# FFN's side 12 in two pieces: one k tile at the weights' place modulo 256 bytes, three 192 bytes beyond

## The chip, the core and the metric

The kernel runs on one core of a Trainium2 chip. The core has TensorE (PE, the matrix engine; its loads of the stationary operand are listed apart as PEld), VectorE (DVE), ScalarE (ACT), GpSimd (POOL) and SyncE (SP, which only issues transfers). Data lie in SBUF, 128 partitions wide, and matmul results in PSUM banks. The metric is the device time of one execution in microseconds; a time before the change is the median of three runs.

## The reference

A trunk of four layers over 512 positions and 1024 channels, in float32. Each layer adds a mixer and then a gated feed-forward network (FFN) to `x`:

```python
for layer in range(DEPTH):                      # DEPTH = 4
    h = rmsnorm(x, norm_mix[layer])
    # layers 0 and 3: s5_mixer; 1: gla_mixer; 2: diff_attn_mixer
    x = x + mix
    h = rmsnorm(x, norm_ffn[layer])
    x = x + swiglu_ffn(h, ffn_w_gate_up[layer], ffn_w_down[layer])
return rmsnorm(x, norm_final)

def swiglu_ffn(h, w_gate_up, w_down):
    g, u = jnp.split(h @ w_gate_up, 2, axis=-1)  # 1024 x (2 x 2816)
    return (jax.nn.silu(g) * u) @ w_down         # 2816 x 1024
```

The change is in `h @ w_gate_up` of all four layers.

## The kernel before

**Numbers in two parts.** A float32 product is made of three matmuls in the format `float32r`: each operand is split into a high part (a cast on ACT) and a low part (a subtraction on DVE), and high x high, high x low and low x high are summed in PSUM. For weights this is `high` (line 405) and `low` (line 413), which fill one of five buffers `whl`. One matmul takes a stationary operand of 128 x 128, loaded just before it, and a moving operand of 256 or 512 columns.

**The FFN's first product with seven multiplications.** `h` transposed and the weights are each taken as 2 x 2 blocks, and the product is made by a scheme with seven block products in place of eight (Strassen's kind). The 2816 hidden columns go in 11 blocks of 256 (`seven_block`). A block takes seven products with the names `one` to `seven`. Each product has 24 matmuls (line 576): two column halves `j`, four k tiles of 128, and the three part products, with the weights stationary and a *side* moving, 256 columns wide. Sides are sums of quarters of `h`: "11" and "12" are quarters themselves, "1", "2", "3", "4" and "22" are others or sums. Products `one`, `six`, `seven` and `four` write the PSUM bank `a`, `five` and `three` bank `c`, and `two`, the only one that reads side "12", writes `d`, a bank of another group (`sbank`, tag "s"). From block 2 on the order in a block is `one`, `five`, `six`, `two`, `seven`, `three`, `four`.

**Where sides lie.** Sides "11" and "12" lie in one tile `sides` of 4160 float32 columns. It is a slot of the pool `hp`, of 16,640 bytes a partition, which is 65 x 256, so that both slots of that pool start at the same place modulo 256. In the tile, side "11" starts at column 48 (192 bytes) and side "12" at column 2112 (8448 bytes, 33 x 256). Each holds high and low part (`z`), four k tiles and 256 columns; the steps between these are multiples of 256 bytes. The other five sides have tiles of their own, in the FFN's pool. The pieces of `whl` that are loaded as weights all start at multiples of 256 bytes from its start.

**How sides 11 and 12 are made.** While the mixer before the FFN ends, `Sides.take` scales each half tile of `x` with the gains, PE transposes it, and `keep` copies it (line 196) into the tile `halves`. When the second of the four position tiles is in, `parts` splits the quarter: a cast on ACT (line 192) and a subtraction on DVE (line 193), each of 128 x 1024. This happens twice per layer, for "11" and for "12".

**The order of work.** The first two blocks of an FFN follow a plan that is written out (the string `plan` in `ffn`: products of block `a` and `b`, splits of weights, sums of sides); there, and in the last steps of the mixer that lead to it, every engine's order is by hand (`hand_all`). From there on (`hand()`) a planner orders the instructions by their place in the program and the costs it assumes. After three or four blocks a group ends, and `gemm_b` (lines 433 to 435) multiplies the activations of the group with the down projection, 512 columns wide, into the banks `acc`. In layer 0 groups have 3, 3, 3 and 2 blocks, in the others 4, 4 and 3. The attention's own value projection has a 256-column form of its own (`values_of`, line 2378), in which `hT` is stationary and `whl` moves, into banks `acc`.

Weights come by DMA, 512 KB at a time, issued on SP, and where a sum of two quarters is wanted, a second one is added by a DMA of POOL (line 612).

Of the kernel before, what the change touches and what calls it, by code (L numbers as in the profile page):

```python
# [12 lines left out]
F32 = mybir.dt.float32  # L13
# [4 lines left out]
ALU = mybir.AluOpType  # L18
# [50 lines left out]
class Left:  # L69
# [15 lines left out]
    def room(self):  # L85
        self.hT = [self.tr.hp.tile([P, KT, SEQ], F32R, tag="hT", name=f"hT{z}") for z in range(2)]
# [67 lines left out]
class Sides(Left):  # L154
# [6 lines left out]
    def room(self):  # L161
        F = self.tr.hp.tile([P, 4, 4, 256], F32, tag="hT", name="halves")
        self.whole = F
        self.F = {(0, 0): F[:, 0], (1, 0): F[:, 1], (0, 1): F[:, 2], (1, 1): F[:, 3]}

        two = self.tr.hp.tile([P, 4096 + 64], F32R, tag="hT", name="sides")
        at = lambda n: two[:, n : n + 2048].rearrange("p (z k n) -> p z k n", z=2, k=4)
        self.place = {"11": at(48), "12": at(2112)}
        self.heads = []

    def quarter(self, q, half, b):
# [15 lines left out]

        return [self.F[k] for k in ((0, 0), (0, 1), (1, 0), (1, 1))]

    def parts(self, name, src, ks=slice(0, 4)):  # L190
        o = self.place[name][:, :, ks]
        self.tr.nc.scalar.copy(o[:, 0], src)
        self.tr.nc.vector.tensor_tensor(o[:, 1], src, o[:, 0].bitcast(F32), op=ALU.subtract)

    def keep(self, t, d, p):
        self.tr.nc.scalar.copy(self.F[t // 2, d][:, :, (t % 2) * P : (t % 2 + 1) * P], p[:])
# [129 lines left out]
class Trunk:  # L326
# [236 lines left out]
        return evac  # L563


    def seven_product(self, side, w, bank, first, hl=None):

        if hl is None:
            hl = self.halves(w, 4, 256)
        mm = self.nc.tensor.matmul  # L570
        for j in range(2):
            c = slice(j * P, (j + 1) * P)
            o = bank[:, j * 256 : (j + 1) * 256]
            for k in range(4):
                for n, (x, y) in enumerate(((0, 0), (0, 1), (1, 0))):
                    mm(  # L576
                        o, hl[:, x, k, c], side[:, y, k], start=first and not (j or k or n),
                        stop=k == 3 and n == 2, skip_group_check=True,
                    )

    def seven_block(self, fp, slots, left, wgu, b, turn, na):
# [1 line left out]

        nc = self.nc
        v = nc.vector
        A = left.place
        T = lambda name: fp.tile([P, 512], F32, tag="r1" if name == "r1" else "glu", name=name, bufs=2 if name == "r1" else 3)
        W, H, bank, keep, lent = {}, {}, {}, {}, set()
        if b < 2:
# [40 lines left out]
        def room1(room=None):  # L630
            load("1", 0, 1, (0, 0), room)

        def room22(room=None):
            load("22", 1, 1, None, room)
# [2 lines left out]
            load("3", 0, 1, (1, 1))  # L637

        def product(side, name, bank, first):
            self.seven_product(A[side], W.get(name), bank, first, H.pop(name, None))  # L640

        def one():
            bank["a"] = self.acc("a")
            product("11", "11", bank["a"], True)
# [5 lines left out]
        def two():  # L650
            bank["d"] = self.sbank("d")
            product("12", "21", bank["d"], True)
# [7 lines left out]
        def five():  # L660
            bank["c"] = self.acc("c")
            product("1", "1", bank["c"], True)
# [59 lines left out]
    def ffn(self, l, left, after=None, turn=False, aside=None, small=None):  # L722
# [7 lines left out]
        with self.tc.tile_pool(name=f"ffn{l}", bufs=1, reuse_waits="tile") as fp:  # L730
# [6 lines left out]
            if glued:  # L737
                lent = room()
# [1801 lines left out]
```

## Time and profile before

| | |
|---|---|
| median of 3 runs | 2264.95 us (2261.33 to 2266.5) |
| the profiled execution | 2264.01 us |
| its span, first to last instruction | 2262.1 us |
| mean granted TensorE clock | 0.996 |
| busy: PE, DVE, ACT, POOL | 97%, 70%, 49%, 14% |
| matmuls of line 576 in all four layers | 7392, of which 1056 read side 12 |

One execution was recorded with the profiler. A row of a group of instructions gives its line, engine and operation, the tiles written and read (`d<-sides,whl`), the shape, the count, then busy time in us, mean duration in ns, and the idle time of the engine ahead of it with what ended most of it. A row of the timeline gives start, us from start to last end, engine, line, tiles and count. A row of the chain gives the start, the length and the work that the end of the kernel is followed back to. Times are from the span's start. Ends of matmuls are modelled, and matmuls overlap.

### The profile page before, as it was taken

Reading aid. Unit: us, or ns where it says so; the run is one execution under the profiler, and the core shown is the slowest. Engines: PE = TensorE matmul, PEld = TensorE weight load, DVE = VectorE, ACT = ScalarE, POOL = GpSimd, SP = SyncE. Lnnn points to the kernel's source line nnn. Section 1 sums busy time; section 2 is a strip of 40 time slices with the busy share of each in tenths; the row PEclk is TensorE's granted clock in tenths of the full one; section 3 lists DMA queues with packets and bytes.
Section 4 is the critical chain, followed back from the end, with each engine's and each line's share of the span. In section 5 each row is a group of like instructions: output and inputs, shape, how many; then the busy total and the mean of one; then the engine's idle time right before and its main releaser. Section 6 shows DMA issues by size and latency. Waiting matters only on the chain.

```text
span 2262.1 us, 37360 instructions
## 1 busy us (share of the span) xinstructions
PE 2191.7 (97%) x14967; PEld 1963.9 (87%) x14967; DVE 1580.2 (70%) x2411; ACT 1111.5 (49%) x1773; POOL 317.9 (14%) x432
## 2 busy tenths in 40 slices
PE   6999999999999999999999999999999899999998
PEld 5888889989777799998988888989998788989997
DVE  9955878776535488776745676967766965957675
ACT  8534535444443365564435676644544234635443
POOL 4301141431000010100002231101000000101000
PEclk9999999999999999999999999999999999999999
DMA  4356666763322566765237465985641546766632
GB/s 89 65 170 167 172 159 176 173 172 100 106 76 74 149 158 178 180 172 154 94 137 149 100 152 138 237 212 134 174 99 50 153 146 155 198 160 161 165 75 75
DMA packets 295527, 319.92 MB, mean 141 GB/s; under 512 B 70141, under 2 KB 235289, under 8 KB 295226
## 3 DMA queue, kind: packets, MB, share of 16 engines
q1 hardware_dynamic: 232730, 235.79, 34.5%
q0 software_dynamic: 62624, 81.75, 19.5%
q8 instruction: 118, 1.93, 0.4%
q14 instruction: 55, 0.45, 0.1%
HBM read 285.62 MB, written 16.65 MB: 134 GB/s over the span
## 4 chain that ended last, share of the span: by engine, by line
PE 48%; DVE 3%; ACT 2%; issue 1%; DMA 1%; POOL 0%; DVEq 0%; POOLq 0%; ACTq 0%; SPq 0%
PE a L576 10%; PE acc L433 8%; PE acc L435 8%; PE acc L434 8%; PE c L576 5%; PE d L576 3%; PE y L1481 1%; PE op L2323 1%; PE s L2290 1%; DVE whl L413 1%; PE acc L2378 1%; ACT whl L405 1%; PE V L1445 1%; PE tp L116 0%; DMA wst<-in_ffn_w_gate_up_dram 0%
## 5 line engine op out<-in xcount | busy, mean ns | idle before, releaser
L413 DVE TENSOR_TENSOR whl<-wst,whl 128x1024 fp32r<-128x1024 f32 x272 | 331.6, 1223 | 276.9 <-ACT whl L405 276.2
L405 ACT CAST whl<-wst 128x1024 fp32r<-128x1024 f32 x272 | 284.6, 1051 | 339.7 <-PE acc L435 250.3
L576 PE MATMUL a<-side,whl 128*128 128x256 f32 x3168 | 383.9, 277 | 6.9 <-DVE whl L413 6.0
L576 PEld LDWEIGHTS a<-side,whl 128*128 128x128 f32 x3168 | 371.0, 188 | 9.2 <-DVE whl L413 6.7
L433 PE MATMUL acc<-whl,act 128*128 128x512 f32 x704 | 276.4, 393 | 1.7 <-DVE g L621 1.2
L434 PE MATMUL acc<-whl,act 128*128 128x512 f32 x704 | 275.0, 391 | 0.0
L435 PE MATMUL acc<-whl,act 128*128 128x512 f32 x704 | 274.9, 390 | 0.0
L576 PE MATMUL c<-side,whl 128*128 128x256 f32 x2112 | 255.2, 277 | 3.3 <-DVE whl L413 3.3
L576 PEld LDWEIGHTS c<-side,whl 128*128 128x128 f32 x2112 | 247.0, 188 | 4.2 <-DVE whl L413 4.1
L413 DVE TENSOR_TENSOR whl<-slot,whl 128x1024 fp32r<-128x1024 f32 x105 | 127.7, 1221 | 67.3 <-ACT whl L405 66.9
L433 PEld LDWEIGHTS acc<-whl,act 128*128 128x128 f32 x704 | 132.5, 188 | 30.8 <-DVE g L621 1.7
L435 PEld LDWEIGHTS acc<-whl,act 128*128 128x128 f32 x704 | 132.4, 188 | 27.6
L405 ACT CAST whl<-slot 128x1024 fp32r<-128x1024 f32 x105 | 110.0, 1052 | 92.5 <-PE acc L435 41.2
L434 PEld LDWEIGHTS acc<-whl,act 128*128 128x128 f32 x704 | 132.4, 188 | 26.4 <-issue 0.2
L576 PE MATMUL d<-sides,whl 128*128 128x256 f32 x1056 | 133.7, 283 | 2.5 <-ACT whl L405 2.5
L576 PEld LDWEIGHTS d<-sides,whl 128*128 128x128 f32 x1056 | 128.9, 191 | 3.3 <-ACT whl L405 3.3
L576 PE MATMUL a<-sides,whl 128*128 128x256 f32 x1056 | 129.3, 278 | 1.2 <-DVE whl L413 1.2
L433 PE MATMUL acc<-whl,hT 128*128 128x512 f32 x320 | 128.6, 402 | 0.0
L576 PEld LDWEIGHTS a<-sides,whl 128*128 128x128 f32 x1056 | 125.2, 188 | 2.4 <-DVE whl L413 1.4
L435 PE MATMUL acc<-whl,hT 128*128 128x512 f32 x320 | 125.3, 392 | 0.0
L434 PE MATMUL acc<-whl,hT 128*128 128x512 f32 x320 | 125.3, 391 | 0.0
L612 POOL DMA_DIRECT2D wst<-in_ffn_w_gate_up_dram x44 | 57.0, 1295 | 443.9 <-DMA wst<-in_ffn_w_gate_up_dram 222.7
(456 smaller groups left out, 3935.1 us busy)
## 6 DMA issues: line engine op xcount, KB each, us to landing
wst<-in_ffn_w_gate_up_dram SPq DMA_DIRECT2D x88, 512.0 KB, 4.6
wst<-in_ffn_w_down_dram SPq DMA_DIRECT2D x88, 512.0 KB, 4.4
slot<-in_ffn_w_gate_up_dram SPq DMA_DIRECT2D x69, 512.0 KB, 5.7
wst<-in_ffn_w_gate_up_dram POOLq DMA_DIRECT2D x44, 512.0 KB, 6.2
halves<-in_ffn_w_gate_up_dram SPq DMA_DIRECT2D x42, 512.0 KB, 5.0
wst<-in_s_w_glu_dram SPq DMA_DIRECT2D x32, 512.0 KB, 4.9
wst<-in_gla_w_in_dram SPq DMA_DIRECT2D x24, 512.0 KB, 3.7
wst<-in_diff_w_qkv_dram SPq DMA_DIRECT2D x24, 512.0 KB, 4.6
```

The source lines that it names most:

```text
L405: self.last["high"] = self.nc.scalar.copy(hl[:, 0], w[:])
L413: self.last["low"] = self.nc.vector.tensor_tensor(hl[:, 1], w[:], hl[:, 0].bitcast(F32), op=ALU.subtract)
L433: mm(out, lh, rh, start=first, stop=False)
L434: mm(out, lh, rl, start=False, stop=False)
L435: self.last["mm"] = mm(out, ll, rh, start=False, stop=last)
L576: mm(o, hl[:, x, k, c], side[:, y, k], start=first and not (j or k or n), stop=k == 3 and n == 2, skip_group_check=True,)
L612: nc.gpsimd.dma_start(w[:], left.quarter(*plus, b), accum_op=ALU.add)
L1445: mm(V[kk][z][:, bs(b)], inm[:, z, bs(b)], U[:, bs(b)], start=True, stop=True)
L1481: mm(yb[:, b], q[:, j, b], om[:, j // 2, bs(b)], start=False, stop=j == 3)
L2290: nc.tensor.matmul(ss[m][:], qs[:, m, ts], ks[:, m, z], start=z == 0, stop=z == 1)
L2323: nc.tensor.matmul(op[:, 0], aT[:, kt], vall[0][:, kt, j * P : (j + 1) * P], start=kt == 0, stop=kt == 3)
L2378: nc.tensor.matmul(o, stat(k, x, t), hl[:, y, a], start=not (k or t % 2 or n), stop=k == KT - 1 and n == 2, skip_group_check=True,)
```

## The change

Side 11 moves to column 560 of its tile (2240 bytes, 8 x 256 + 192). Side 12 is stored in two pieces: k tile 0 at column 0 (512 columns: high and low part), and k tiles 1 to 3 at column 2608 (10,432 bytes, 40 x 256 + 192; 1536 columns). `parts` makes it with one cast and one subtraction for each piece, both casts ahead of both subtractions. The products fetch a moving slice through a new function `row`, which picks the piece by k tile. Nothing is changed in the attention: its order of before, which the change's title calls mended, is in both kernels.

```diff
         two = self.tr.hp.tile([P, 4096 + 64], F32R, tag="hT", name="sides")
-        at = lambda n: two[:, n : n + 2048].rearrange("p (z k n) -> p z k n", z=2, k=4)
-        self.place = {"11": at(48), "12": at(2112)}
+        at = lambda n, k=4: two[:, n : n + 512 * k].rearrange("p (z k n) -> p z k n", z=2, k=k)
+        self.place = {"11": at(560)}
+        self.split12 = [(slice(0, 1), at(0, 1)), (slice(1, 4), at(2608, 3))]
...
-    def parts(self, name, src, ks=slice(0, 4)):
-        o = self.place[name][:, :, ks]
-        self.tr.nc.scalar.copy(o[:, 0], src)
-        self.tr.nc.vector.tensor_tensor(o[:, 1], src, o[:, 0].bitcast(F32), op=ALU.subtract)
+    def parts(self, name, src):
+        pieces = self.split12 if name == "12" else [(slice(0, 4), self.place[name])]
+        for ks, o in pieces:
+            self.tr.nc.scalar.copy(o[:, 0], src[:, ks])
+        for ks, o in pieces:
+            self.tr.nc.vector.tensor_tensor(o[:, 1], src[:, ks], o[:, 0].bitcast(F32), op=ALU.subtract)
+
+    def row(self, name, z, k):
+
+        if name != "12":
+            return self.place[name][:, z, k]
+        return self.split12[0][1][:, z, 0] if k == 0 else self.split12[1][1][:, z, k - 1]
...
-    def seven_product(self, side, w, bank, first, hl=None):
+    def seven_product(self, row, w, bank, first, hl=None):
...
-                        o, hl[:, x, k, c], side[:, y, k], start=first and not (j or k or n),
+                        o, hl[:, x, k, c], row(y, k), start=first and not (j or k or n),
...
-        A = left.place
...
         def product(side, name, bank, first):
-            self.seven_product(A[side], W.get(name), bank, first, H.pop(name, None))
+            row = lambda y, k: left.row(side, y, k)
+            self.seven_product(row, W.get(name), bank, first, H.pop(name, None))
```

## Prediction

> **What bounds the kernel now.** I read the page first: the span, the busy shares, the chain that ended last and the costliest groups. The columns of a group are its instructions, then busy us and mean ns of one, then the idle time before them.
>
> ```profile
> span 2262.1 us, 37360 instructions
> PE 2191.7 (97%) x14967; PEld 1963.9 (87%) x14967; DVE 1580.2 (70%) x2411; ACT 1111.5 (49%) x1773; POOL 317.9 (14%) x432
> PE 48%; DVE 3%; ACT 2%; issue 1%; DMA 1%; POOL 0%; DVEq 0%; POOLq 0%; ACTq 0%; SPq 0%
> L576 PE MATMUL d<-sides,whl 128*128 128x256 f32 x1056 | 133.7, 283 | 2.5 <-ACT whl L405 2.5
> ```
>
> TensorE (PE) is busy 97% of the span, and nearly all of the chain that the profile could follow is PE. `d` is the bank of product `two`, the only product that reads side 12; there are 44 of them (1056 / 24). Where they stand I read from stretches that hold whole FFN blocks from the third on; of nine such stretches (29 of the 44 `d` lie in them) here are the first and the sum:
>
> ```profile
> core 0: us, PE busy (x) PEld busy (x) DVE busy (x) ACT busy (x) POOL busy (x), PEclk, DMA share, GB/s
> 323.85:381.80 57.95, 57.95 (x506) 57.95 (x505) 44.66 (x50) 32.30 (x40) 6.42 (x7) 1.00 0.72 188
> ...
> sum 560.49, PE 560.49 PEld 560.44 DVE 428.31 ACT 300.63 POOL 45.14; mean PE 62.28 PEld 62.27 DVE 47.59 ACT 33.40 POOL 5.02
> ```
>
> PE is busy in all of the 560.49 us, at clock 1.00, and VectorE (DVE) in 76%. So a nanosecond saved per matmul here is a nanosecond of the kernel until DVE is late, which has a quarter of the time to spare. The timeline of PE shows what a matmul costs. The start of one product minus the start of the next is the figure to trust, since durations overlap (2.88 us of records in 2.72 us):
>
> ```profile
> 323.62 0.39 PE L435 MATMUL acc<-whl,act 128*128 128x512 f32 x1
> 323.85 2.99 PE L576 MATMUL a<-sides,whl 128*128 128x256 f32 x24
> 326.68 2.99 PE L576 MATMUL c<-side,whl 128*128 128x256 f32 x24
> 329.50 2.99 PE L576 MATMUL a<-side,whl 128*128 128x256 f32 x24
> 332.33 3.04 PE L576 MATMUL d<-sides,whl 128*128 128x256 f32 x24
> 335.20 2.90 PE L576 MATMUL a<-side,whl 128*128 128x256 f32 x24
> 337.94 2.88 PE L576 MATMUL c<-side,whl 128*128 128x256 f32 x24
> ...
> 348.82 2.88 PE L576 MATMUL a<-side,whl 128*128 128x256 f32 x24
> 351.54 3.02 PE L576 MATMUL d<-sides,whl 128*128 128x256 f32 x24
> 354.40 2.90 PE L576 MATMUL a<-side,whl 128*128 128x256 f32 x24
> 357.14 1.07 PE L576 MATMUL c<-side,whl 128*128 128x256 f32 x8
> ```
>
> Three paces are in it. A product takes 2.72 us (348.82 to 351.54; 113.3 ns a matmul): **fast**. After the wide `acc` matmuls the same products take 2.83 us (323.85 to 326.68; 117.8 ns): **slow**, and they stay so, product after product, until a `d` comes. `d` takes 2.86 us (351.54 to 354.40; near 120 ns), and the product behind it 2.74. After every whole `d` the pace is fast, also where it was slow before. So `d` does two things: it costs 2.86 + 2.74 - 2 x 2.72 = 0.16 us more than two fast products, and it ends the slow pace.
>
> By the code, side 12 begins 2112 x 4 = 8448 = 33 x 256 bytes into its tile, the place of the weights modulo 256 by the change's own words; side 11 begins 192 bytes beyond, and runs at the fast or the slow pace. That the place is what costs has a second witness. In the attention, line 2378 multiplies `hT` and `whl` slices that both start at their tiles' place (all steps are multiples of 256 bytes), and it writes `acc` banks. Its median is that of `d`, where the fast products have 276 (second row):
>
> ```profile
> L2378 PE MATMUL acc<-whl,hT x192: 274/283/365, 1281.6 to 1337.6; 128*128 128x256 f32 x192
> L576 PE MATMUL a<-sides,whl x1056: 276/276/384, 214.2 to 2205.3; 128*128 128x256 f32 x176
> ```
>
> **The change part by part.**
>
> *Product `two`.* Of 24 matmuls, the 6 of k tile 0 (three in each column half) stay at the weights' place; 18 go 192 bytes beyond. 24 matmuls at the place cost 0.16 us, 6.7 ns each; so 6 cost 0.04 us if the cost goes with their number. Saved per `d`: 0.12 us. The ends: 0.16 if three in a row are too few to build the delay up, 0.08 if each first half leaves the nine matmuls behind it slow (9 x 4.5 ns).
>
> *Which of the 44 count.* The 29 in the nine stretches do. Of the 7 `d` of the blocks just ahead of these, I count the 5 of layers 0, 1 and 3. Two come early in each layer, under the written plan. There the chain of layer 3 reads:
>
> ```profile
> 1923.11 5.74 PE d L576 x48
> ...
> 1937.03 0.91 PE rows L147 x8
> ...
> 1939.09 0.96 ACT whl L405
> ```
>
> Both `d` are on it: ScalarE (ACT) waits for `rows` behind them, and DVE for ACT. I count 6 for layers 0, 1 and 3, whose plan is the same. In layer 2 the chain is on DVE there, so its 2 plan `d`, and the 2 of its next blocks, among waits on DVE and weights, count nothing:
>
> ```profile
> 1415.27 3.49 DVE whl L413 x3
> 1418.75 1.22 DVE s L208 x2
> ```
>
> Together 29 + 5 + 6 = 40. Gain: 40 x 0.12 = 4.8 us; ends 34 x 0.08 = 2.7 and 40 x 0.16 = 6.4.
>
> *Splitting side 12 in two pieces.* Once per layer one ACT cast and one DVE subtract of 1024 columns become two each, of 256 and 768: 4 + 4 more instructions. What an extra one costs comes from the same operations at two sizes:
>
> ```profile
> L192 ACT CAST sides<-halves 128x1024 fp32r<-128x1024 f32 x8 | 8.4, 1049 | 0.2
> L713 ACT CAST act<-r 128x512 fp32r<-128x512 f32 x66 | 41.0, 621 | 75.7 <-DVE r L694 59.9 <-DVE r L703 15.8
> L226 DVE TENSOR_TENSOR side<-s,side 128x512 fp32r<-128x512 f32 x8 | 5.1, 684 | 0.0
> L193 DVE TENSOR_TENSOR sides<-halves,sides 128x1024 fp32r<-128x1024 f32 x8 | 9.8, 1223 | 3.2 <-ACT sides L192 3.2
> ```
>
> ACT: 2 x 621 - 1049 = 193 ns; DVE: 2 x 684 - 1223 = 145 ns. Against it stands that DVE today waits for the cast (3.2 us in all, last row) and can begin on the small piece some 0.7 us earlier. Queued behind the pieces are ACT's square and copy of the next half tile and DVE's additions into `x`; behind these wait the transposes, and PE meanwhile has accumulation and the first products to do. Side 12 itself is wanted only at the first `d`, in layer 3 at 1923, two products after the last accumulation. Ends: 0.8 us gained (3.2 us of waits, a quarter saved) and 4 x (0.193 + 0.145) = 1.4 us lost; I take 0.1 lost, since four waits and eight added instructions about balance. Without that cover it would be the 1.4.
>
> *The rest.* Side 11 moves by 512 x 4 = 2048 bytes and keeps its place modulo 256: nothing. `row` only picks slices while the program is written: no instruction. No DMA is added or moved, so SP's and POOL's queues issue what they did. The tile keeps its 4160 columns, so no other tile moves.
>
> *The sum.* The profiled execution took 2264.01 us: span 2262.1 and 1.9 around it. 2264.01 - 4.8 + 0.1 = 2259.3. It lies 0.94 under the median of the runs, 2264.95; I give the time on the median's footing: **2260.2 us**. Its own ends: 2264.95 - 6.4 - 0.8 = 2257.7 and 2264.95 - 2.7 + 1.4 = 2263.7. A measurement of this kernel tells about 0.2%, 4.5 us, from no change: the gain stands at that bound.
>
> **The rivals.**
>
> *One k tile is too short to end the slow pace.* This is the one on the other side. In the trace the slow pace ends after 24 matmuls at the weights' place, never after three. If three don't do it, each of the nine stretches stays slow to its end once an accumulation has made it so. They hold 147 products behind their first `d` that are not `d` (75 in five of three blocks, 63 in three of four blocks, 9 in one of two). At 2.83 - 2.72 = 0.106 us (24 x 4.44 ns): +15.6. The `d` themselves still save 0.04 each, -1.6. Time: 2264.95 + 14 = **2279**. It decides as soon as a third of these products stay slow. For it speaks how lasting both paces are; what a short spell does, two places show that are alike, in layers 1 and 3, where two `d` matmuls precede 22 of `a`:
>
> ```profile
> 849.28 0.50 PE L576 MATMUL d<-sides,whl 128*128 128x256 f32 x2 [0.44 <-ACT whl L405]
> 849.62 2.84 PE L576 MATMUL a<-side,whl 128*128 128x256 f32 x22
> 852.29 2.79 PE L576 MATMUL d<-sides,whl 128*128 128x256 f32 x22
> ...
> 1966.82 0.50 PE L576 MATMUL d<-sides,whl 128*128 128x256 f32 x2 [0.44 <-ACT whl L405]
> 1967.16 2.77 PE L576 MATMUL a<-side,whl 128*128 128x256 f32 x22
> 1969.76 2.78 PE L576 MATMUL d<-sides,whl 128*128 128x256 f32 x22
> ```
>
> The 22 take 2.67 us in the one and 2.60 in the other, slow and fast: either can follow. Against the rival: each `d` gets two spells, and in the row of 332.33 the whole price of 2.87 us is there without a gentle onset.
>
> *A short spell throws the fast pace into the slow one, too.* Then nearly all products turn slow: of the 264 that are not `d`, 225 are fast now (counted by their starts), and I take 190 as on the path, without those in the stretches where DVE leads. 190 x 0.106 - 1.6 = +18.5: **2283**. It needs that no spell of three ends well, so it is the rarer.
>
> *Half of each `d` goes slow, and its second spell mends it:* 0.08 saved, 40 x 0.08 = 3.2: **2261.8**.
>
> *The place is not what costs.* `two` is also the only product in an `s` bank. Then the change does nothing: 2264.95 to +1.4, about **2265**. Against it: the row of line 2378, with the same 283 in `acc` banks. The Trainium skill's page "SBUF — State Buffer", section "Who interferes with whom", stands with this rival: it gives TensorE two independent read ports, one for the moving operand and one for LDWEIGHTS, and lets engines contend only at the port pair that VectorE and GpSimd share. By that rule the sum would be no gain at all. The trace doesn't agree: 113.3, 117.8 and 120 ns for one shape.
>
> *The planner orders something else differently,* since four pairs of instructions are new to it: some us either way, unseen here.
>
> **How the numbers follow.** My forecast 0.55 (0.38 of it beyond 0.2%, as its middle lies on the bound and 0.12 is a middle value); too short 0.19; thrown into slow 0.10; mended half 0.07; the place not at fault 0.03; the order 0.06 (0.01 faster, 0.01 within, 0.04 slower). Faster 0.39, within 0.28 (0.17 + 0.07 + 0.03 + 0.01), slower 0.33. The range goes from the lower end of the forecast, 2257.5, over the first rival to 2280; beyond it lie the second, 0.10, and a little on both sides. The forecast's own range is 2257.7 to 2263.7.
>
> **What would show it.** Right: in the stretch from 323.85, `d` to the next start 2.76 instead of 2.87 and 2.86; every product behind it 2.72; median of the `d` matmuls near 276; still 2.83 for the three products after an accumulation. Wrong: 2.83 also behind a `d` (first rival), 2.83 right after fast products (second), `d` unchanged (the place). Also wrong if PE shows idle time in the nine stretches, or if ACT and DVE run other instructions between 1400 and 1500 than now.

## The result, and the profile after

| | before | after |
|---|---|---|
| median of 21 runs each | 2265.18 us (2261.04 to 2267.33) | 2260.2 us (2257.55 to 2263.78) |
| the profiled execution, its span | 2264.01, 2262.1 us | 2262.09, 2260.1 us |

The ratio is 0.9982, with a 95% interval of 0.9976 to 0.9989: 2.5 to 5.4 us are saved. The profiled executions differ by only 1.9 us. In the one of after, ACT's cast of side 11, the first instruction on the tile that the change rearranges, starts at 172.32 us against 171.03 before, and the first product `two` at 221.59 against 220.34: some 1.3 us were lost ahead of anything that the change touches. Single executions scatter like that, and the stretches below are compared instead of the spans.

The page of the changed kernel has these rows on what the prediction spoke of (lines of the FFN are 9 higher):

```profile
span 2260.1 us, 37368 instructions
PE 2185.5 (97%) x14967; PEld 1957.2 (87%) x14967; DVE 1578.0 (70%) x2415; ACT 1111.5 (49%) x1777; POOL 318.1 (14%) x432
L585 PE MATMUL d<-sides,whl 128*128 128x256 f32 x1056 | 129.2, 278 | 2.5 <-ACT whl L414 2.5
```

Four more instructions on ACT and four on DVE, and PE busy 6.2 us less. The matmuls of `d` take 278 ns in the mean where they took 283. The timeline of PE at the same place in the program as in the prediction:

```profile
323.90 0.40 PE L444 MATMUL acc<-whl,act 128*128 128x512 f32 x1
324.14 2.90 PE L585 MATMUL a<-sides,whl 128*128 128x256 f32 x24
326.88 2.88 PE L585 MATMUL c<-side,whl 128*128 128x256 f32 x24
...
348.68 2.88 PE L585 MATMUL a<-side,whl 128*128 128x256 f32 x24
351.40 2.92 PE L585 MATMUL d<-sides,whl 128*128 128x256 f32 x24
354.16 2.88 PE L585 MATMUL a<-side,whl 128*128 128x256 f32 x24
356.88 2.88 PE L585 MATMUL c<-side,whl 128*128 128x256 f32 x24
...
427.88 2.93 PE L585 MATMUL d<-sides,whl 128*128 128x256 f32 x24
430.66 2.88 PE L585 MATMUL a<-side,whl 128*128 128x256 f32 x24
433.38 0.84 PE L585 MATMUL c<-side,whl 128*128 128x256 f32 x6
```

A `d` takes 2.76 us from its start to the next (351.40 to 354.16), and the product behind it 2.72 at once: 0.12 us less for the two. The `d` at 427.88 is the first behind an accumulation; it takes 2.78 and the product behind it 2.72, so one k tile at the weights' place ends the slow pace. This stretch at 324.14 happened to begin fast; the next, at 419.40, began slow as before. The nine stretches, taken from the start of the first product to the start of the first accumulating matmul, sum to this in the windows of before, and below it in those of after:

```profile
sum 559.86, PE 559.86 PEld 559.84 DVE 427.68 ACT 300.38 POOL 45.14; mean PE 62.21 PEld 62.20 DVE 47.52 ACT 33.38 POOL 5.02
```

```profile
sum 555.76, PE 555.76 PEld 555.74 DVE 424.99 ACT 299.65 POOL 42.75; mean PE 61.75 PEld 61.75 DVE 47.22 ACT 33.29 POOL 4.75
```

4.1 us less, and PE still busy in all of it. And the pieces of side 12, in the groups of ACT and DVE:

```profile
L194 ACT CAST sides<-halves 128x768 fp32r<-128x768 f32 x4 | 3.3, 831 | 0.0
L194 ACT CAST sides<-halves 128x256 fp32r<-128x256 f32 x4 | 1.6, 407 | 0.1
L196 DVE TENSOR_TENSOR sides<-halves,sides 128x1024 fp32r<-128x1024 f32 x4 | 4.9, 1221 | 1.1 <-ACT sides L194 1.1
L196 DVE TENSOR_TENSOR sides<-halves,sides 128x768 fp32r<-128x768 f32 x4 | 3.8, 953 | 0.6 <-ACT sides L194 0.6
L196 DVE TENSOR_TENSOR sides<-halves,sides 128x256 fp32r<-128x256 f32 x4 | 1.7, 422 | 0.8 <-ACT sides L194 0.7
```

Two pieces cost ACT 407 + 831 - 1049 = 189 ns and DVE 422 + 953 - 1223 = 152 ns more, once per layer; DVE's waits for these casts sank from 3.2 to 2.4 us. The order of the instructions is otherwise that of before on every engine.

### The profile page after: what moved, and what is told of

It is laid out like the page before. It is cut to its first block, busy times and chain, and to the rows that moved or that the text cites. A ratio compares the mean times of both kernels' runs of the same rounds, so it can differ in the third digit from the quotient of the medians.

```text
span 2260.1 us, 37368 instructions
## 1 busy us (share of the span) xinstructions
PE 2185.5 (97%) x14967; PEld 1957.2 (87%) x14967; DVE 1578.0 (70%) x2415; ACT 1111.5 (49%) x1777; POOL 318.1 (14%) x432
## 4 chain that ended last, share of the span: by engine, by line
PE 83%; DVE 7%; ACT 4%; issue 3%; DMA 2%; SPq 1%; POOL 0%; DVEq 0%; POOLq 0%; ACTq 0%
PE a L585 17%; PE acc L442 13%; PE acc L444 13%; PE acc L443 13%; PE c L585 9%; PE d L585 5%; PE y L1490 2%; DVE whl L422 2%; ACT whl L414 1%; PE op L2332 1%; PE s L2299 1%; PE tp L116 1%; PE V L1454 1%; PE acc L2387 1%; DMA wst<-in_ffn_w_down_dram 1%
```

## The experiments

The theory: matmuls whose moving operand lies at the weights' place modulo 256 bytes cost 6.7 ns each, and they are also what ends the slow pace that the wide accumulating matmuls leave. The first rival says that something else in product `two` ends it, the second that the two pieces, not the place, make the gain. All edits are against the changed kernel, and all of these kernels have its order of instructions on every engine, apart from the pieces (and one more semaphore instruction on GpSimd where side 11 is split). "The weights' place" is a place by the code: the traces hold no addresses, and in every run only the moving operand is shifted while the weights stay. So the runs show what the moving operand's start modulo 256 bytes does; that it counts against the weights, and not by itself, they don't show.

**All of side 12 beyond.**

```diff
-        self.place = {"11": at(560)}
-        self.split12 = [(slice(0, 1), at(0, 1)), (slice(1, 4), at(2608, 3))]
+        self.place = {"11": at(48), "12": at(2096)}
```

(`parts` and `row` then treat side 12 like side 11.)

> Side 12 in one piece, all of it 192 bytes beyond the weights' place (it starts at column 2096 in place of 2112; side 11 stays). Theory (matmuls at the weights' place cost 6.7 ns each, and are also what ends the slow pace): product two costs 2.72 us on the fast pace, but once a wide accumulation has made the pace slow, it stays slow to the end of the stretch: 2.83 us for every product there. 40 x 0.16 saved, 147 x 0.106 and 29 x 0.106 lost: +12.3, about 2277. Rival (the pace is ended by something else in product two, such as its PSUM bank): all products behind a d stay at 2.72 us, and 6.4 us are saved, about 2259.

In what the chip runs, this differs from the kernel of before by one number, 2096 for 2112. Measured: 2280.7 us against 2268.36 of before on that chip, 12.3 us slower by the medians and 13.8 by the ratio of 1.0061 (1.0049 to 1.0074). Its timeline of PE:

```profile
324.43 0.39 PE L441 MATMUL acc<-whl,act 128*128 128x512 f32 x1
324.66 2.99 PE L582 MATMUL a<-sides,whl 128*128 128x256 f32 x24
...
333.14 2.99 PE L582 MATMUL d<-sides,whl 128*128 128x256 f32 x24
335.96 2.99 PE L582 MATMUL a<-side,whl 128*128 128x256 f32 x24
338.79 2.99 PE L582 MATMUL c<-side,whl 128*128 128x256 f32 x24
341.62 2.99 PE L582 MATMUL a<-side,whl 128*128 128x256 f32 x24
```

`d` takes 2.82, its neighbours 2.83: the slow pace goes through `d` and stays to the end of the stretch. The nine stretches sum to 573.88 us, 14.0 more than before; 147 products and the 29 `d` at 0.106 more, and 29 x 0.16 less, make 14.0. So the old place, 64 bytes further on, carries a cost and a service, and the service is the larger. The first rival falls: same product, same bank, no end of the slow pace.

**Two pieces, both at the place.**

```diff
-        self.split12 = [(slice(0, 1), at(0, 1)), (slice(1, 4), at(2608, 3))]
+        self.split12 = [(slice(0, 1), at(0, 1)), (slice(1, 4), at(2624, 3))]
```

> Side 12 in two pieces as in the change, but both pieces at the weights' place: the four more casts and subtractions alone. Theory: product two stays at 2.86 us, the time within 0.5 us of the kernel before, about 2265. Rival (the two pieces and not the place make the gain): about 2260.

2267.89 against 2268.36 us, ratio 1.0000 (0.9991 to 1.0009). `d` takes 2.86 us and the product behind it 2.74, as before:

```profile
351.88 3.02 PE L585 MATMUL d<-sides,whl 128*128 128x256 f32 x24
354.74 2.90 PE L585 MATMUL a<-side,whl 128*128 128x256 f32 x24
357.48 0.73 PE L585 MATMUL c<-side,whl 128*128 128x256 f32 x5
```

The eight added instructions cost nothing that this can resolve (the interval is 2 us to either side), and the pieces alone don't make the gain: the second rival falls.

**Only the low part of k tile 0 at the place.** High and low part of that tile become two places; the low one keeps column 0.

```diff
-        self.split12 = [(slice(0, 1), at(0, 1)), (slice(1, 4), at(2608, 3))]
+        one = lambda n: two[:, n : n + 256].rearrange("p (k n) -> p k n", k=1)
+        rest = at(2608, 3)
+        self.split12 = [(slice(0, 1), (one(304), one(0))), (slice(1, 4), (rest[:, 0], rest[:, 1]))]
```

(`parts` and `row` take the high and the low place from these pairs.)

> As the change, but of k tile 0 only the low part at the weights' place: 2 of 24 matmuls, one in each half, in place of 6. Theory (6.7 ns for each, and one ends the slow pace): product two 2.733 us, 40 x 0.147 = 5.9 saved against the kernel before, about 2259.3. Rival (one matmul is too short a spell to end the slow pace): the stretches stay slow behind a d at 2.83 us a product, about 2277.

2263.07 against 2268.36 us, ratio 0.9982 (0.9973 to 0.9991).

```profile
351.66 2.94 PE L588 MATMUL d<-sides,whl 128*128 128x256 f32 x24
354.44 2.88 PE L588 MATMUL a<-side,whl 128*128 128x256 f32 x24
357.16 1.07 PE L588 MATMUL c<-side,whl 128*128 128x256 f32 x8
```

A half hit. A lone matmul ends the slow pace too: behind every whole `d` of the stretches the products take 2.72 us. There are two of them in a `d`, twelve matmuls apart, and the first is enough: the `d` entered from the slow pace at 427.66 takes 2.78 us, where twelve more matmuls at the slow pace would add about 0.05 (an estimate, 12 x 4.4 ns). But `d` does not take 2.733. The rows give 2.78, and the nine stretches more exactly 2.77: they sum to 556.44 us, 0.36 more than in the second profile of the change (below), so 0.012 more for each of 29 `d` (one stretch began fast in either). Two lone matmuls cost 0.05 us, some 27 ns each, more than the change's six. The price of 6.7 ns does not hold for a spell of one, and nothing is won by shortening it.

**Two k tiles at the place.**

```diff
-        self.place = {"11": at(560)}
-        self.split12 = [(slice(0, 1), at(0, 1)), (slice(1, 4), at(2608, 3))]
+        self.place = {"11": at(1072)}
+        self.split12 = [(slice(0, 2), at(0, 2)), (slice(2, 4), at(3120, 2))]
```

(`row` then picks piece `k // 2` and its tile `k % 2`.)

> As the change, but k tiles 0 and 1 of side 12 at the weights' place: 12 of 24 matmuls, two spells of six. Theory (each matmul at the place costs 6.7 ns): product two 2.80 us on the fast pace, 40 x 0.08 = 3.2 us saved against the kernel before, ratio 0.9986. Rival, formed on the run with the low part alone, whose two single matmuls cost more than the change's six (the price is for each spell, some 20 to 30 ns, and not for each matmul): product two 2.76 to 2.78 us, the ratio that of the change, 0.998.

2263.0 against 2268.59 us, ratio 0.9978 (0.9968 to 0.9988).

```profile
349.76 2.96 PE L585 MATMUL d<-sides,whl 128*128 128x256 f32 x24
352.56 2.88 PE L585 MATMUL a<-side,whl 128*128 128x256 f32 x24
355.28 0.96 PE L585 MATMUL c<-side,whl 128*128 128x256 f32 x7
```

`d` takes 2.80 us: 0.08 more than a fast product, as the price per matmul had it, and not as the rival had it. So 6, 12 and 24 matmuls cost 0.04, 0.08 and 0.16. The nine stretches agree: 557.23 us here, 556.08 in the second profile of the change, 1.15 apart, and 29 x 0.04 is 1.16. The time doesn't resolve this: the interval holds the expected 0.9986, and the ratio of the change as well.

**64 and 128 bytes beyond,** each measured once, with side 12 in one piece:

```diff
+        self.place = {"11": at(2096), "12": at(16)}    # 64 bytes beyond; at(32): 128
```

(The line stands in place of the change's two; `parts` and `row` again treat side 12 like side 11.)

> Side 12 in one piece, 64 bytes beyond the weights' place (column 16; side 11 at column 2096, 192 beyond as before). Theory (only the same place costs and ends the slow pace): as with all of side 12 192 bytes beyond, product two at the pace it finds, 2.72 or 2.83 us, and the slow pace kept behind it; about 2277. Rival (the distance in steps of 64 bytes matters, and 192 is not like 64): product two at another pace of its own, or ending the slow pace at no price, which would be 2258 to 2259.

> Side 12 in one piece, 128 bytes beyond the weights' place (column 32; side 11 at column 2096). Theory and rival as for 64 bytes: 2.72 or 2.83 us and the slow pace kept, about 2277; or a pace of its own.

At 64 bytes the time was 2278.45 us, near the 2277 expected, and the nine stretches sum to 573.89 us, as at 192: they are slow throughout, and `d` stays slow in them. But 64 bytes is not like 192. Under the written plan of layer 0, two `d` follow the same product `a`. At 192 bytes, with all of side 12 beyond, they run at the fast pace:

```profile
217.81 2.98 PE L582 MATMUL a<-sides,whl 128*128 128x256 f32 x24
220.63 5.60 PE L582 MATMUL d<-sides,whl 128*128 128x256 f32 x48
226.07 5.60 PE L582 MATMUL c<-side,whl 128*128 128x256 f32 x48
```

At 64 bytes they don't:

```profile
217.24 2.98 PE L582 MATMUL a<-sides,whl 128*128 128x256 f32 x24
220.06 5.82 PE L582 MATMUL d<-sides,whl 128*128 128x256 f32 x48
225.71 5.61 PE L582 MATMUL c<-side,whl 128*128 128x256 f32 x48
```

The two take 5.44 us in the first and 5.65 in the second, 2.72 and 2.83 each; the `a` ahead takes 2.82 in both, of which one gap of 0.2 us is no part of its pace (its other matmuls start 113 ns apart). In this trace no `d` runs at 2.72, whatever came ahead. So the theory's "pace it finds" fails at 64 bytes, and of the rival the part holds that product two has a pace of its own; that pace happens to be the slow one, which is why the time came out as expected. Behind these two `d` the pace is fast again, behind those of the stretches slow; what 64 bytes does to the pace behind is not settled.

At 128 bytes the time was 2271.72 us, the stretches sum to 565.88 us, and the expectation was wrong. The timeline of PE there:

```profile
347.94 2.88 PE L582 MATMUL a<-side,whl 128*128 128x256 f32 x24
350.66 3.01 PE L582 MATMUL d<-sides,whl 128*128 128x256 f32 x24
353.51 2.99 PE L582 MATMUL a<-side,whl 128*128 128x256 f32 x24
356.34 2.99 PE L582 MATMUL c<-side,whl 128*128 128x256 f32 x24
...
367.65 2.99 PE L582 MATMUL a<-side,whl 128*128 128x256 f32 x24
370.47 3.01 PE L582 MATMUL d<-sides,whl 128*128 128x256 f32 x24
373.32 2.91 PE L582 MATMUL a<-side,whl 128*128 128x256 f32 x24
376.07 2.88 PE L582 MATMUL c<-side,whl 128*128 128x256 f32 x24
```

`d` takes 2.85 us here too, and it turns the pace over: fast ahead of 350.66 and slow behind it (2.83), slow ahead of 370.47 and fast behind it (2.75, then 2.72). In all nine stretches each `d` does so. That a spell of three throws the fast pace into the slow one was the prediction's second rival; a whole product does it, at this place.

**The spell in product `one`.** The names are exchanged: side 11 in two pieces, side 12 whole and 192 bytes beyond.

```diff
-        self.place = {"11": at(560)}
+        self.place = {"12": at(560)}
-        pieces = self.split12 if name == "12" else [(slice(0, 4), self.place[name])]
+        pieces = self.split12 if name == "11" else [(slice(0, 4), self.place[name])]
-        if name != "12":
+        if name != "11":
```

> The names exchanged: side 11 in two pieces with its k tile 0 at the weights' place, all of side 12 192 bytes beyond. Product one, the first of each block, then makes the spell. Theory (a spell of three ends the slow pace wherever it stands): product one 2.76 us, two 2.72; behind an accumulation the slow pace ends in product one and not only in two, three products earlier, 9 x 0.3 = 2.7 us more than the change: about 2257.5. Rival (straight behind the wide matmuls a spell does not end the pace): the first block of each stretch stays slow, 9 x 4 x 0.106 = 3.8 us worse than the change, about 2264.

2259.29 against 2268.36 us, ratio 0.9968 (0.9955 to 0.9980).

```profile
419.31 0.39 PE L444 MATMUL acc<-whl,act 128*128 128x512 f32 x1
419.54 2.93 PE L585 MATMUL a<-sides,whl 128*128 128x256 f32 x24
422.31 2.88 PE L585 MATMUL c<-side,whl 128*128 128x256 f32 x24
425.03 2.88 PE L585 MATMUL a<-side,whl 128*128 128x256 f32 x24
427.75 2.88 PE L585 MATMUL d<-sides,whl 128*128 128x256 f32 x24
```

Straight behind the accumulation `one` takes 2.77 us and everything behind it 2.72, `d` too. So the rival falls here. The nine stretches sum to 553.49 us, 6.4 less than before. Beside the changed kernel on one chip:

> The changed kernel once more, beside the next one on the same chip. Theory: ratio to the kernel before 0.998 (40 x 0.12 us saved).

> The kernel with k tile 0 of side 11 at the weights' place and all of side 12 192 bytes beyond, beside the change. Theory (three slow products less in each of nine stretches): 2.5 to 2.9 us less than the change, ratio to the kernel before 0.9967. Rival (the difference to the change seen before was the chip's): the same time as the change.

| | median | ratio to before (2266.37 us) | sum of the nine stretches |
|---|---|---|---|
| the change | 2261.64 us | 0.9977 (0.9968 to 0.9986) | 556.08 us |
| spell in `one` | 2258.26 us | 0.9961 (0.9948 to 0.9975) | 553.51 us |

3.4 us lie between the medians where 2.5 to 2.9 were expected, 2.57 of them in the nine stretches. The intervals overlap a little, so the whole time alone doesn't settle it. The sum of the stretches does: it is the same twice (553.49 and 553.51), against 555.76 and 556.08 of the change. This version beats the kernel before by its whole time, and the change by its stretches.

## Why the prediction was right, point by point

*The bound.* That a nanosecond of a matmul in the nine stretches is a nanosecond of the kernel held: PE is busy in all of each of them, in every kernel above, at clock 1.00, and DVE never became late (busy 425 of 556 us).

*Product `two`.* 0.12 us per `d` was forecast and measured: 2.76 and 2.72 where there were 2.86 and 2.74, and the median of its matmuls sank from 283 to 276 ns. The value between the ends was taken on the ground that the cost goes with the number of matmuls at the place. That holds for 6, 12 and 24 (spells of three, of six and of the whole product), but not for lone ones.

*The count.* 29 x 0.12 = 3.5 us were to lie in the nine stretches. The second profile of the change has 559.86 - 556.08 = 3.78 there, the first 4.1. What is beyond 3.5 comes from stretches that began on the fast pace (0.3 us each, as the one at 324.14), which was not foreseen. Of the rest, the plan of layer 3 shows its part. In the chain there, `d` to `rows` took 1937.03 - 1923.11 = 13.92 us, and after the change:

```profile
1922.43 5.52 PE d L585 x48
...
1936.11 0.91 PE rows L147 x8
...
1938.17 0.96 ACT whl L414
```

13.68 us, and ACT follows 2.06 us behind `rows` in both: 0.24 for two `d`, as counted. For the other `d` that I counted the profiles say less. From the start of an FFN's first product to that of its first stretch, layer 3 took 126.43 us before, 125.98 and 126.09 in the two profiles of the change, which fits three `d` at 0.12. Layer 1 took 127.09 before (799.33 to 926.42), 127.15 and 127.38 after: its three counted `d` are not seen there. In layer 0 it was 109.60, then 108.64 and 108.73, and with both pieces at the place, where nothing should change, 110.12; the scatter is larger than the term. So the count of 40 is shown for the 29 in the stretches and for layer 3, and is open for the rest. The whole, 4.98 us between the medians and 4.1 by the ratio, is consistent with the 4.8.

*The number.* That the median is the forecast 2260.2 to the last digit is luck: the interval leaves 2.5 to 5.4 us of gain, two of nine stretches began fast without being forecast, and some counted terms are not seen.

*The two pieces.* The added durations (189 and 152 ns) were forecast as 193 and 145, and DVE's waits shrank by the 0.8 us named as the other end. Two pieces at one place measured no difference, to 2 us either way. That agrees with "about balanced", but would also agree with the ends, 0.8 gained or 1.4 lost.

*The rivals.* One k tile is long enough to end the slow pace; but the rival's price was real, as the kernel with no tile at the place shows: 14.0 us in the stretches, the time 12.3 us slower by the medians. A short spell of three does not throw the pace over; a whole product 128 bytes beyond does. Half-slow `d` do not occur: they would take 2.80 us, and take 2.76. The place is what costs: the same product in the same bank took 2.86 us at the place, 2.72 or 2.83 at 192 bytes beyond, 2.83 at 64 and 2.85 at 128. So the rule in the Trainium skill's page "SBUF — State Buffer", section "Who interferes with whom", that TensorE's two reads are independent, is not enough to tell the time of these pairs. Whether the two reads meet, or the start of the moving operand counts by itself, is open, as said above. The planner moved nothing.

*Chances.* I gave 0.33 to slower, largely because the trace of before had no spell of three matmuls. The row that I read as "no gentle onset" (the `d` at 332.33, entered from the slow pace) pointed the right way, though it shows no spell of three.

## What to carry to other kernels

Measure matmuls by start to start over whole products: here one shape runs at 113.3, 117.8 or 120 ns by where its moving operand starts modulo 256 bytes, with the weights at 0, and by what ran before. A placement that looks merely slow may be doing a service to what follows, so ask what state it leaves behind before removing it; here removing it whole lost 12 to 14 us and removing three quarters gained 4 to 5. And once it is known what the service is, put it where it is needed first: the same spell in the first product behind the accumulation gained 2.6 us more in the stretches.

## What was not expected of the hardware

- The pace is a state that lasts: 147 products in the nine stretches of the kernel without a spell stay at 2.83 us a product until the stretch ends, and one matmul at the weights' place (some 27 ns) is enough to bring 2.72 us back.
- At 192 bytes beyond the weights' place a product keeps whichever pace it finds, 2.72 or 2.83 us; at 64 (one run) it takes 2.83 behind either. At 0 and 128 bytes (one run) it takes 2.86 and 2.85 us; 0 leaves the fast pace, 128 turns fast into slow and slow into fast.
- A lone matmul at the weights' place costs some 27 ns, and one of a spell of three, six or twenty-four 6.7 ns.

Why the wide accumulating matmuls nearly always leave the slow pace (in 74 of the 81 stretches of the nine profiles without the spell in `one`), and what the two paces are inside TensorE, is not settled: no run here looked below the starts of instructions. Nor was the weights' own start ever moved. A kernel that makes the spell only in the first block of each stretch was not tried either: it needs a second copy of one k tile, 512 columns, and `sides` has 64 to spare.
